# Output projection in another pass order, decode attention per key/value pair, and a wider warm-up, in one hybrid trunk layer

## The chip, the cores and the metric

The kernel runs on one core of a Trainium2 chip. TensorE multiplies (its weights are loaded by a queue of its own, PEld), VectorE (DVE), ScalarE (ACT) and GpSimd (POOL) do the elementwise work, and DMA queues, most of them issued from SyncE (SP), bring weights from HBM. The metric is the device time of one execution in microseconds; the median of three runs before the change is 2037.36 us (2037.23 to 2038.41).

## The reference

One layer for 256 prompt tokens and 8 sample tokens (one each of 8 sequences), 264 columns together:

```python
x = x + 0.5 * swiglu(rmsnorm(x, n1), f1g, f1u, f1d)          # FFN1, d_ff 5504
proj = rmsnorm(x, nm) @ w_in                                  # 2048 -> q, k, v and RWKV columns
o_att, k_buf, v_buf = attend(q, k, v, sinks)                  # 16 query heads, 4 kv heads of 64
o_rwkv, shift, S = rwkv_time_mix(proj[..., ATT_COLS:], shift0, wkv0, ...)   # 16 heads of 64
x = x + concatenate([o_att, o_rwkv]) @ w_out
x = x + 0.5 * swiglu(rmsnorm(x, n2), f2g, f2u, f2d)          # FFN2
y = rmsnorm(x, final_norm)
```

For the prompt, `attend` is sliding-window attention (window 128) with a relative bias per head and a sink per head:

```python
s = einsum('...qhgd,...khd->...hgqk', q, k) * 64**-0.5 + bias
m = maximum(max(s), sink);  p = exp(s - m)
o = einsum('...hgqk,...khd->...qhgd', p / (sum(p) + exp(sink - m)), v)
```

For the sample tokens the same formula runs against a cache of 128 keys and values per sequence, with the token's own key and value appended as column 129 (`swa_decode`). `rwkv_time_mix` is a recurrence with a 64x64 state per head, a group norm per head and a gate.

## The kernel before

Activations lie transposed: a tile is 128 features by 264 tokens. The model width has 16 tiles (`KD`), the FFN 43, the input projection 38. Each large product ("GEMM") is done in two-part fp32: `chunk` (L116-125) loads 256 KB of weights by SP, ACT casts them to `hi` (L123), DVE subtracts to `lo`; then three matmuls of 128x264 per 128x128 weight block go into an accumulator `acc` (three PSUM buffers, `NACC`). The raw weights have a ring of six, `hi` and `lo` rings of four. All other matmuls write to "m" banks (five, `mp()`).

The program is written as generator tasks: `spawn` makes one, `tick` (called by `gemm` between weight blocks) steps the open tasks, `drain(list)` steps until the tasks of the list are done. A scheduler then orders each engine's instructions; each engine runs its own order from first to last, and so do the DMA queues. What is queued behind a waiting instruction waits too.

The mixing stage runs in the order of `SEQ`: four batches of RWKV heads ("b", two pairs of heads each), keys and values ("kv"), then eight query tiles q0 to q7. The work that runs beside the input projection and after it:

- `chain`, one per batch: a triangular solve in 32 steps (DVE on X and Xt), a round trip of Xt through DRAM (`sb`, then `TT`), small matmuls (names TN, zs, W, BT, gm, uv, N, S), and at the end `gnorm`, a group norm with a Sqrt on ACT and two reciprocals on DVE. Batch b gives the mixed tiles 2b and 2b+1.
- `attend(t, q)` (L712-753), one per query tile t: for each of two heads, matmuls of scores, a custom DVE step that adds the bias and takes the maximum (L730), `softmax` (L701-710: exponentials on ACT, the sum and the division on DVE), then three transposes (L739-741), and the product with the values. Tile t gives mixed tile 8+t; p = t // 4 is the key/value pair.
- `dec_attend(att)` (L755-819), one task for all sample tokens, spawned after q7: scores with cached keys as weights and padded queries of 8 columns as moving data, the softmax of 129 columns, values likewise; at the end it waits for all eight attention tasks and copies its columns into the mixed tiles 8 to 15 by POOL (L818).

The output projection (L867-881) goes over the 16 mixed tiles in passes, given by the table `PASS` (L40): tiles 0-3, then 4-7, then 8-15. Before each pass `drain(need(ks))` completes what its tiles depend on; `split` casts the tiles to `hi` and subtracts `lo` (L857-861); for each of 16 output blocks one accumulator then takes 3 matmuls for every tile of the pass, and DVE adds it to the residual `xr`. The last pass hands its sums to FFN2. `need` (L863) counts any tile above 7 as needing all attention tasks and the decode.

At the very start TensorE runs 14 fp32 matmuls of 128x128 on a tile of ones (`NWARM`), which need only a memset.

Of the kernel before, what the change touches and what calls it, by code (L numbers as in the profile page):

```python
# [7 lines left out]
F32 = mybir.dt.float32  # L8
# [22 lines left out]
NWARM = 14  # L31
# [8 lines left out]
PASS = [[0,1,2,3],[4,5,6,7],[8,9,10,11,12,13,14,15]]  # L40
# [3 lines left out]
NVEC = 155  # L44
# [3 lines left out]
def body(tc, I, O):  # L48
# [24 lines left out]
    def mm(out, lhsT, rhs, start=True, stop=True, **k):  # L73
        TE.matmul(out, lhsT, rhs, start=start, stop=stop, **k)  # L74
# [20 lines left out]
    with ExitStack() as ctx:  # L95
# [17 lines left out]
        def mp():  # L113
            return pp.tile([P, 512], F32, tag="m", bufs=NM, name=uid("m"))
# [37 lines left out]

        warm = mp()
        for _ in range(NWARM):
            mm(warm[:, :P], ones, ones)
# [176 lines left out]
        def mixing_body(mx, n2, n3, XD):  # L332
            def fix(shape, name):
                return mx.tile(list(shape), F32, name=name)
# [23 lines left out]
            qd = fix((P, 2, NB, 4), "qd")  # L358
# [353 lines left out]
            def attend(t, q):  # L712
                p = t // 4
                G.tensor_copy(qd[:, p, :, t % 4], q[:, NP:T])
# [40 lines left out]
            def dec_attend(att):  # L755
                yield
                qb = tmp((P, 2, NB, 2, 4))
                G.memset(qb, 0.0)
                for h in range(2):
                    r = HALF[h]  # L760
                    G.tensor_copy(qb[r, :, :, h, :], qd[r])
                yield
                sps = mp()
                sv = sps[:, :P].rearrange("p (h x) -> p h x", h=2)
                for p in range(2):
                    for b in range(0, NB, 2):
                        kc = load(I["kc"][p, b // 2], (P, 2, P))
                        for j in range(2):
                            c0 = p * 32 + (b + j) * 4
                            mm(sv[:, :, c0:c0 + 4], kc[:, j, :], qb[:, p, b + j])  # L770
                st = tmp((P, P))
                A.copy(st, sps[:, :P])
                pr = tmp((P, 2, NB, 4))
                for p in range(2):
                    tt(G, pr[:, p], qd[:, p], bc(kT[p][:, NP:T].unsqueeze(2), (P, NB, 4)), ALU.mult)
                yield
                s2 = mp()
                TE.transpose(s2[:, 0:P], st, ident)
                for h in range(2):
                    r = HALF[h]  # L780
                    mm(s2[r, P:P + 1], pr[r], ones[r, 0:1])
                bd = load(I["bd"], (P, 129))
                s = tmp((P, 129))
                mxv = ring((P, 2), "mxv", 6)
                V.tensor_tensor_reduce(out=s, in0=s2[:, 0:129], in1=bd, op0=ALU.add, op1=ALU.max, scale=1.0,
                                       scalar=vc(VSD), accum_out=mxv[:, 0:1])
                softmax([s], mxv, vc(VSD), 1)
                dg = tmp((P, P))
                ts(V, dg, ident, s[:, P:P + 1], ALU.mult)
                yield  # L790
                tp = mp()
                TE.transpose(tp[:, 0:P], s[:, 0:P], ident)
                pt = tmp((P, P))
                A.copy(pt, tp[:, 0:P])
                pn = mp()
                for h in range(2):
                    r = HALF[h]
                    mm(pn[r, 0:64], ones[:, 0:64], dg[:, r])
                od = tmp((P, 2, NB, 4))
                for p in range(2):  # L800
                    tt(V, od[:, p], pn[:, p * 32:p * 32 + 32].rearrange("p (b i) -> p b i", i=4),
                       bc(vT[p][:, NP:T].unsqueeze(2), (P, NB, 4)), ALU.mult)
                yield
                op = mp()
                ov, pv = (x[:, :P].rearrange("p (h x) -> p h x", h=2) for x in (op, pt))
                for b in range(NB):
                    vcache = load(I["cv"][b], (P, 256))
                    for p in range(2):
                        c0 = p * 32 + b * 4
                        mm(ov[:, :, c0:c0 + 4], vcache[:, p * P:(p + 1) * P], pv[:, :, c0:c0 + 4])  # L810
                of = od.rearrange("p a b i -> p (a b i)")
                for h in range(2):
                    r = HALF[h]
                    tt(V, of[r], ov[r, h, :], of[r], ALU.add)
                while any(g in tasks for g in att):
                    yield
                for t in range(8):
                    G.tensor_copy(mixed[8 + t][:, NP:T], od[:, t // 4, :, t % 4])  # L818
# [5 lines left out]
            bat, att, bts = [], [], []  # L824
            for kind, i in SEQ:
# [10 lines left out]
                elif kind == "kv":  # L836
                    w, p = i // 2, i % 2
                    ps = win(LKV + i)
                    x = slot()
                    (kT, vT)[w][p] = x  # L840
                    with tc.high_priority():
                        tt(V, x, ps[:, :T], rs, ALU.mult)
                    spawn(kvtask(w, p, x))
                else:
                    ps = win(LKV + 4 + i)
                    q = slot(tag="o")
                    with tc.high_priority():
                        stt(q, ps[:, :T], 0.125, rs, ALU.mult, ALU.mult)
                    att.append(spawn(attend(i, q)))
                    if len(att) == 8:  # L850
                        att.append(spawn(dec_attend(list(att))))
# [11 lines left out]
            def need(ks):  # L863
                return [g for i, g in enumerate(bat) if any(k // 2 == i for k in ks)] + (att if max(ks) > 7 else [])
# [93 lines left out]
def layout(i):  # L958
# [3 lines left out]
    for n in (1, 2):  # L962
# [9 lines left out]
    heads = np.array([(2 * p + h) * 4 + j for h in range(2) for p in range(2) for b in range(NB) for j in range(4)])  # L972
# [4 lines left out]
        np.broadcast_to(i["attn_sinks"][0], (P, 16)), i["attn_sinks"][0][heads][:, None]], 1))  # L977
# [20 lines left out]
    a["kc"] = c(ck.reshape(4, 2, P, 2, P).transpose(3, 0, 4, 1, 2))  # L998
# [30 lines left out]
```

## Time and profile before

| | |
|---|---|
| median of 3 runs | 2037.36 us |
| profiled execution, span | 2034.2 us |
| DVE, ACT, POOL busy | 1324.9, 1035.9, 241.2 us |
| HBM read, written | 347.25 MB, 10.21 MB |
| first projection matmul | 1099.96 us |
| first FFN2 matmul into an "m" bank | 1268.07 us |

The profile is one execution. Its span is the device work of that execution and is 3.2 us shorter than the median, which is taken around the whole launch. The views used are the page (busy time by engine, the chain of waits that ended last), the timeline of an engine (start, duration, engine, line, operation, out<-in, form, count), and busy times by stage. In a stage's row stand the stretch, its length, the busy time and count of each engine, the clock that TensorE was granted (1.00 is full), the busy share of the DMA engines and GB/s.

### The profile page before, as it was taken

The page shows a single profiled execution, that of the slowest core. Times are in us where ns is not written, and L with a number is a line of the kernel's source. Part 1 is how long each engine was busy: PE and PEld are TensorE (multiplying, and loading weights), DVE is VectorE, ACT ScalarE, POOL GpSimd, SP SyncE. Part 2 cuts the span into 40 slices and gives each one's busy share as a digit, 9 for nine tenths or more (in the row PEclk, how much of TensorE's full clock was granted, in tenths as well). Part 3 has the DMA queues.
Part 4 walks back from the last instruction along what each step waited for, and adds up shares of the span by engine and source line. Part 5 has one row for each costly group of instructions (what it writes and reads, how often), then busy time and mean ns, then how long its engine had stood idle before and what let it go on. Part 6 is the DMA issues. An engine that isn't in the chain of part 4 may idle for free.

```text
span 2034.2 us, 45416 instructions
## 1 busy us (share of the span) xinstructions
PE 2000.0 (98%) x17096; PEld 1963.2 (97%) x17096; DVE 1324.9 (65%) x2647; ACT 1035.9 (51%) x2027; POOL 241.2 (12%) x337
## 2 busy tenths in 40 slices
PE   9999999999999999999999999999999999999998
PEld 9999999999999999999898789999999999999998
DVE  5865555655555577678778756775666666666665
ACT  5644444444444466665555534554444444444445
POOL 0301001020110122120100000120101101010012
PEclk9999999999999999999999979999999999999999
DMA  6566565655556576554455335465565565656654
GB/s 228 177 187 197 180 195 186 187 184 176 186 171 191 181 208 204 153 153 125 138 146 165 101 108 180 172 183 177 191 182 193 182 189 187 189 191 180 194 182 145
DMA packets 227421, 358.39 MB, mean 176 GB/s; under 512 B 42352, under 2 KB 80768, under 8 KB 227200
## 3 DMA queue, kind: packets, MB, share of 16 engines
q1 hardware_dynamic: 220752, 346.95, 54.7%
q10 hardware_dynamic: 6448, 8.53, 1.3%
q8 instruction: 134, 2.20, 0.4%
q14 instruction: 87, 0.71, 0.1%
HBM read 347.25 MB, written 10.21 MB: 176 GB/s over the span
## 4 chain that ended last, share of the span: by engine, by line
PE 93%; DVE 3%; DMA 1%; ACT 1%; issue 1%; SPq 1%; ACTq 0%; DVEq 0%
PE acc L74 84%; PE m L74 8%; DVE lo L58 1%; DMA raw<-in_win 1%; ACT t L68 0%; DVE y L58 0%; ACT L68 0%; DVE st L58 0%; DVE Xt L58 0%; DVE t L678 0%; DMA ld<-in_sT 0%; ACT hi L123 0%; DMA raw<-in_gu 0%; SPq L544 0%; PE m L496 0%
## 5 line engine op out<-in xcount | busy, mean ns | idle before, releaser
L58 DVE TENSOR_TENSOR lo<-raw,hi 128x512 fp32r<-128x512 f32 (+1 forms) x1288 | 869.8, 679 | 549.0 <-ACT hi L123 522.3
L123 ACT CAST hi<-raw 128x512 fp32r<-128x512 f32 (+1 forms) x1288 | 776.4, 607 | 865.1 <-PE acc L74 777.2
L74 PE MATMUL acc<-s,hi 128*128 128x264 f32 x5940 | 1109.8, 286 | 3.9 <-ACT hi L123 2.1
L74 PEld LDWEIGHTS acc<-s,hi 128*128 128x128 f32 x5940 | 923.7, 189 | 11.3 <-ACT hi L123 2.5
L74 PE MATMUL acc<-s,lo 128*128 128x264 f32 x2970 | 847.9, 286 | 4.4 <-DVE lo L58 4.4
L74 PEld LDWEIGHTS acc<-s,lo 128*128 128x128 f32 x2970 | 559.8, 189 | 7.7 <-DVE lo L58 5.2
L74 PE MATMUL acc<-t,hi 128*128 128x264 f32 x2752 | 503.0, 284 | 0.0
L74 PEld LDWEIGHTS acc<-t,hi 128*128 128x128 f32 x2752 | 426.3, 188 | 0.0
L74 PE MATMUL acc<-t,lo 128*128 128x264 f32 x1376 | 388.9, 285 | 0.0
L58 POOL TENSOR_TENSOR t<-t,t 128x264 f32<-128x264 f32 (+1 forms) x148 | 150.8, 1019 | 1151.4 <-ACT hi L123 791.1
L74 PEld LDWEIGHTS acc<-t,lo 128*128 128x128 f32 x1376 | 258.4, 188 | 0.1
L74 PE MATMUL acc<-y,hi 128*128 128x264 f32 x648 | 124.5, 285 | 0.0
L74 PEld LDWEIGHTS acc<-y,hi 128*128 128x128 f32 x648 | 101.7, 188 | 0.2
L74 PE MATMUL acc<-y,lo 128*128 128x264 f32 x324 | 92.4, 285 | 0.0
L58 DVE TENSOR_TENSOR t<-acc,t 128x264 f32<-128x264 f32 x156 | 67.4, 432 | 37.0 <-PE acc L74 36.8
L58 POOL TENSOR_TENSOR o<-o,o 128x264 f32<-128x264 f32 x43 | 36.1, 840 | 231.6 <-ACT o L68 227.6
L74 PE MATMUL acc<-o,hi 128*128 128x264 f32 x324 | 63.0, 284 | 0.0
L74 PEld LDWEIGHTS acc<-y,lo 128*128 128x128 f32 x324 | 60.8, 188 | 0.0
L61 DVE SCALAR_TENSOR_TENSOR s<-acc,s 128x264 f32<-128x264 f32 x96 | 40.6, 427 | 15.9 <-PE acc L74 15.5
L74 PEld LDWEIGHTS acc<-o,hi 128*128 128x128 f32 x324 | 50.3, 188 | 0.0
L74 PE MATMUL m<-s,hi 128*128 128x264 f32 x260 | 48.6, 285 | 0.0
L61 DVE SCALAR_TENSOR_TENSOR x<-acc,x 128x264 f32<-128x264 f32 x96 | 40.5, 427 | 10.0 <-PE acc L74 9.6
(236 smaller groups left out, 1301.1 us busy)
## 6 DMA issues: line engine op xcount, KB each, us to landing
raw<-in_gu SPq DMA_DIRECT2D x688, 256.0 KB, 3.3
raw<-in_dn SPq DMA_DIRECT2D x224, 256.0 KB, 2.8
raw<-in_win SPq DMA_DIRECT2D x152, 256.0 KB, 3.4
raw<-in_dn SPq DMA_DIRECT2D x160, 192.0 KB, 2.7
raw<-in_wout SPq DMA_DIRECT2D x64, 256.0 KB, 3.3
xsp<-x ACTq DMA_DIRECT2D x16, 132.0 KB, 3.3
s<-xsp SPq DMA_DIRECT2D x16, 132.0 KB, 4.0
ld<-in_sT SPq DMA_DIRECT2D x16, 128.0 KB, 3.3
```

Source lines behind the costliest of these rows:

```text
L58: return e.tensor_tensor(out=out, in0=a, in1=b, op=op)
L61: return V.scalar_tensor_tensor(out=out, in0=a, scalar=s, in1=b, op0=op0, op1=op1)
L74: TE.matmul(out, lhsT, rhs, start=start, stop=stop, **k)
L123: A.copy(hi[:, :w], raw[:, :w])
```

## The change

Three things are changed.

1. The warm-up: a memset of 640 columns of ones, a DVE copy of 512 of them into a tile of the `hi` ring, and 44 matmuls with 512 to 128 columns each (f32r), instead of 14 fp32 matmuls of 128x128.
2. The pass order: `PASS` is now tiles 0-3 with 8-11, then 4-7, then 12-15, and `need` lists what each tile needs by itself. The first pass needs batches 0 and 1, attention tiles 0-3 and the decode of pair 0; each of its output blocks takes 24 matmuls; the last pass takes 12.
3. The decode attention runs once per key/value pair, as two tasks, with the queries padded to 32 columns as the weights and the cache (128 columns) as the moving data. Cache tiles of a whole pair (512 KB each) are loaded ahead into another ring, for pair 0 after batch 2 and for pair 1 after decode 0 and batch 3. The new value's share is added from a DRAM copy of the new values (`vnd`).

```diff
-NWARM = 14
+WARM = (512,) * 6 + (384,) * 6 + (264,) * 8 + (256,) * 8 + (192,) * 8 + (128,) * 8
-PASS = [[0,1,2,3],[4,5,6,7],[8,9,10,11,12,13,14,15]]
+PASS = [[0,1,2,3,8,9,10,11],[4,5,6,7],[12,13,14,15]]
+        G.memset(C, 1.0)
+        wr = wp.tile([P, CH * P], F32R, tag="hi", bufs=NHL, name=uid("hi"))
+        V.tensor_copy(wr, C[:, :CH * P])
         warm = mp()
-        for _ in range(NWARM):
-            mm(warm[:, :P], ones, ones)
+        for n in WARM:
+            mm(warm[:, :n], wr[:, :P], wr[:, :n])
+                    if w:
+                        A.dma_start(vnd, kvn[w])
+                        while bat[-2] in tasks:
+                            yield
+                        dec_load(0)
...
+            def dec_load(p):
+                dk[p], dv[p] = ring((P, NB, P), "uv", NUV), ring((P, NB, P), "uv", NUV)
...
+                SP.dma_start(dk[p], I["kc"][p])
+                SP.dma_start(dv[p], I["cw"][p])
+                SP.dma_start(db[p], I["bd"][p])
...
+            def dec_attend(p, qs):
+                for i, q in enumerate(qs):
+                    for h in range(2):
+                        G.tensor_copy(qb[p][HALF[h], :, h * 4 + i], q[HALF[h], NP:T])
...
+                for b in range(NB):
+                    g, x = b % 4 * 32, b // 4 * 129
+                    mm(sps[g:g + 32, x:x + P], qb[p][:, b], dk[p][:, b])
+                for b in range(NB):
+                    g, x = b % 4 * 32, b // 4 * 129 + P
+                    mm(sps[g:g + 32, x:x + 1], qb[p][:, b], kT[p][:, NP + b:NP + b + 1])
...
+                softmax([s[:, 0], s[:, 1]], mxv, vc(VSD + p), 2)
...
+                for j in range(2):
+                    TE.transpose(tp[:, j * P:(j + 1) * P], s[:, j, 0:P], ident)
...
+                for b in range(NB):
+                    g, j = b % 4 * 32, b // 4
+                    mm(op[g:g + 32, j * P:(j + 1) * P], pt[:, j, g:g + 32], dv[p][:, b])
+                for j in range(2):
+                    stt(oa[:, j], vr[p][:, j], s[:, j, P:P + 1], op[:, j * P:(j + 1) * P], ALU.mult, ALU.add)
...
+                for i, q in enumerate(qs):
+                    G.tensor_copy(q[:, NP:T], od[:, i])
+                if p == 0:
+                    while bat[-1] in tasks:
+                        yield
+                    dec_load(1)
...
+                    att.append([spawn(attend(i, q))])
+                    if i % 4 == 3:
+                        p = i // 4
+                        d = spawn(dec_attend(p, qs[4 * p:]))
+                        for a in att[4 * p:]:
+                            a.append(d)
             def need(ks):
-                return [g for i, g in enumerate(bat) if any(k // 2 == i for k in ks)] + (att if max(ks) > 7 else [])
+                return [bat[k // 2] for k in ks if k < 8] + [g for k in ks if k > 7 for g in att[k - 8]]
```

How it moves the instructions, at three places. First ACT, around the start of the projection; the casts of L859 (L873 in the changed kernel) make the projection's inputs from the mixed tiles `y`, and the activations with `sta` and `stc` are the exponentials of attention tile 0. Before:

```order
L68 ACTIVATE t_15109<-m_15184,eps 128x264
L123 CAST hi_16571<-raw_16570 128x512
L859 CAST s_16392<-y_12692 128x264
L859 CAST s_16396<-y_12693 128x264
L859 CAST s_16400<-y_13753 128x264
L859 CAST s_16404<-y_13754 128x264
L68 ACT_TABLE_LOAD
L68 ACTIVATE t_15207,stb_15213<-t_15207,sta_15212 128x256
```

and of the change:

```order
L123 CAST hi_16694<-raw_16693 128x512
L68 ACT_TABLE_LOAD
L68 ACTIVATE t_15240,stb_15246<-t_15240,sta_15245 128x256
L68 ACTIVATE t_15241,stb_15246<-t_15241,sta_15245 128x128
L68 ACTIVATE stc_15247<-sta_15245,vec 128x2
L68 ACTIVATE t_15292,stb_15298<-t_15292,sta_15297 128x256
L68 ACTIVATE t_15293,stb_15298<-t_15293,sta_15297 128x128
L68 ACTIVATE stc_15299<-sta_15297,vec 128x2
L873 CAST s_16506<-y_12725 128x264
```

The four casts now stand behind the exponentials of both heads. Second, DVE at the same place: `sta` is the negated maximum that these exponentials take as their bias, and TT is what batch 3's solve brings back from DRAM. Before:

```order
L730 ISA mxv_15261 128x1
L58 TENSOR_TENSOR y_14805<-m_15107,t_15109 128x264
L65 TENSOR_SCALAR sta_15212<-mxv_15209 128x2
L61 SCALAR_TENSOR_TENSOR y_14804<-y_14804,vec,t_12817 128x264
L58 TENSOR_TENSOR Xt_14687<-Xt_14687,st_15249 128x8x2
```

and of the change:

```order
L58 TENSOR_TENSOR y_14838<-m_15141,t_15143 128x264
L58 TENSOR_TENSOR TT_14729<-TT_14729,C 32x8x32
L65 TENSOR_SCALAR sta_15245<-mxv_15242 128x2
L58 TENSOR_TENSOR TT_14729<-TT_14729,C 32x8x32
L61 SCALAR_TENSOR_TENSOR y_14837<-y_14837,vec,t_12850 128x264
L58 TENSOR_TENSOR TT_14729<-TT_14729,C 32x8x32 x2
L65 TENSOR_SCALAR sta_15297<-mxv_15294 128x2
```

The last steps of the solve (Xt) now stand ahead, and the additions on TT have come between the maximum and its negation. Third, TensorE where the first pass goes on after attention tile 3 (rows 8616 on of 15618). Between the first halves of three accumulators and this place stands no GEMM matmul from row 8530 on:

```order
L74 MATMUL m_16118<-sgl,ld_15983 128x264
L74 MATMUL m_16122<-sgl,ld_15985 128x264
L745 MATMUL m_16126<-C,t_15912 128x128
L746 MATMUL m_16126<-C,t_15911 128x128
L747 MATMUL m_16126<-C,t_15911 128x128
L819 MATMUL m_16134<-C,t_16075 128x128 x2
L74 MATMUL m_16177<-t_16062,s_14815 64x256
L74 MATMUL m_16177<-t_16130,s_14815 64x256
L74 MATMUL acc_16538<-s_16522,hi_16570 128x264
L74 MATMUL acc_16618<-s_16522,hi_16694 128x264
L74 MATMUL acc_16718<-s_16522,hi_16742 128x264
```

The rows with `sgl` are the gate of batch 3 behind its group norm, L819 the last transposes of the first decode task; the accumulators' second halves (mixed tiles 8 to 11) follow them. From there to the first FFN2 matmul into an "m" bank stand 768 GEMM matmuls, 348 of them up to the end of the first pass, with attention tiles 4-7 and the second decode task (32 score and value matmuls, transposes) among the 348.

More of the change, by code (lines that the diff above doesn't have):

```diff
@@ L771, in dec_attend @@
[L771 to L775, printed above, removed]
-                yield
[L777 to L782, printed above, removed]
@@ new lines, in dec_attend @@
+                for b in range(NB):
+                    g, x = b % 4 * 32, b // 4 * 129 + P
+                    mm(sps[g:g + 32, x:x + 1], qb[p][:, b], kT[p][:, NP + b:NP + b + 1])
+                dm = ring((P, 768), "bk", 2)
+                s = dm[:, 0:258].rearrange("p (s x) -> p s x", s=2)
+                pt = dm[:, 258:514].rearrange("p (s x) -> p s x", s=2)
+                od = dm[:, 514:546].rearrange("p (i b) -> p i b", i=4)
+                mxv = ring((P, 2), "mxv", 6)
+                for j in range(2):
+                    V.tensor_tensor_reduce(out=s[:, j], in0=sps[:, j * 129:j * 129 + 129], in1=db[p], op0=ALU.add,
+                                           op1=ALU.max, scale=1.0, scalar=vc(VSD + p), accum_out=mxv[:, j:j + 1])
@@ L803, in dec_attend @@
+                A.copy(pt, tp[:, 0:2 * P].rearrange("p (s x) -> p s x", s=2))
                 yield
                 op = mp()
-                ov, pv = (x[:, :P].rearrange("p (h x) -> p h x", h=2) for x in (op, pt))
                 for b in range(NB):
[L807 to L811, printed above, removed]
@@ L812, in dec_attend @@
-                for h in range(2):
[L813 to L818, printed above, removed]
+                    g, j = b % 4 * 32, b // 4
+                    mm(op[g:g + 32, j * P:(j + 1) * P], pt[:, j, g:g + 32], dv[p][:, b])
+                oa = tmp((P, 2, P))
@@ L971, in layout @@
     sc = cols[:NSH * P] - 1536
-    heads = np.array([(2 * p + h) * 4 + j for h in range(2) for p in range(2) for b in range(NB) for j in range(4)])
+    heads = np.array([[(2 * p + min(x // 4, 1)) * 4 + x % 4 for g in range(4) for x in range(32)] for p in range(2)])
     a["vec"] = c(np.concatenate([
```

65 lines of the change are left out of this document (25 added, 40 removed).

## Prediction

> **What bounds the kernel now.** I read the shares by engine first, then the chain of waits, then the busy times by stage. The page's first and fourth parts:
>
> ```profile
> PE 2000.0 (98%) x17096; PEld 1963.2 (97%) x17096; DVE 1324.9 (65%) x2647; ACT 1035.9 (51%) x2027; POOL 241.2 (12%) x337
> PE 93%; DVE 3%; DMA 1%; ACT 1%; issue 1%; SPq 1%; ACTq 0%; DVEq 0%
> ```
>
> TensorE sets the time, and 98% busy leaves 34 us. But a busy TensorE is not one at full rate, so the stages matter. Two rows of the chain give the price of one GEMM matmul (128x264), the second where FFN2 takes over:
>
> ```profile
> 69.33 700.36 PE acc L74 x5760
> 1268.07 7.30 PE m L74 x60
> ```
>
> 700.36/5760 = 0.1216 us. The stretch that the change rearranges runs from the first projection matmul to FFN2's first one at 1268.07. The first is the first row here (timeline); the others are busy times by stage (PE, weight loads, DVE, ACT, POOL, then the granted clock, DMA share and GB/s):
>
> ```profile
> 1099.96 0.93 PE L74 MATMUL acc<-s,hi 128*128 128x264 f32 x4
> ...
> 1099.96:1146.41 46.45, 45.41 (x530) 40.13 (x529) 39.44 (x139) 24.66 (x74) 2.15 (x3) 1.00 0.50 145
> 1146.41:1157.45 11.04, 7.44 (x33) 4.60 (x32) 8.48 (x24) 7.60 (x21) 0.65 (x1) 0.73 0.15 45
> 1157.45:1188.27 30.82, 30.82 (x224) 26.48 (x224) 24.45 (x89) 17.45 (x52) 1.52 (x6) 0.99 0.43 132
> 1188.27:1214.56 26.29, 22.97 (x116) 18.77 (x114) 8.06 (x31) 6.57 (x22) 1.91 (x10) 0.58 0.35 99
> 1214.56:1268.07 53.51, 53.51 (x420) 53.51 (x421) 35.49 (x60) 25.23 (x46) 2.65 (x3) 0.95 0.47 161
> ```
>
> These are 168.1 us for 768 projection matmuls and 36 of the last input projections, 804 in all: 97.8 us at 0.1216. Some 70 us go to attention, batch 3 and decode. Two holes stand out: 11.0 us in which batch 3 reaches its group norm, and 26.3 us in which TensorE is "busy" with the decode's thin matmuls and the last attention tiles at a clock of 0.58. The last row is 420 matmuls in 53.51 us, 0.127 each, because it begins at half clock. The change attacks both holes, and pays for it at the start.
>
> **The warm-up.** Before, TensorE opens with 28 passes of the 14 square matmuls, and DVE is idle until 7.68. Real work is dense from 15.9:
>
> ```profile
> 0.73 0.20 POOL L147 MEMSET ones<- 128x128 f32 x1 [0.29 <-POOLq L1021]
> 0.99 5.12 PE L74 MATMUL m<-ones 128*128 128x128 f32 x28 [0.99 <-POOL eps L150]
> 8.21 1.03 PE L74 MATMUL acc<-s,hi 128*128 128x264 f32 x4 [2.10 <-ACT hi L123]
> ...
> 11.25:15.90 4.65, 4.43 (x35) 1.00 0.97 358
> 15.90:26.10 10.20, 10.20 (x84) 1.00 0.72 214
> ...
> 1106.23 0.11 PE m L740
> 1156.05 0.21 PE m L740
> ```
>
> Up to 15.9, 56 GEMM matmuls are done (4 of them slower), so at the dense pitch of 10.20/84 = 0.1214 the head equals dense work from about 15.9 - 52 x 0.1214 = 9.6. The new warm-up needs a memset of 640 columns (the 128-column one takes 0.20 with its fixed part; about 0.6 by size), then a DVE copy (about 0.5, as a 128x264 step takes 0.4 to 0.5), so it starts near 2.15 rather than 0.99. Its 44 matmuls stream 6x512 + 6x384 + 8x(264+256+192+128) = 12,096 columns; at 264 per 0.12 us that is 5.5 us, 6.1 with a fixed part each, 11.5 if all ran at half clock. The last two rows are one pass of 128 columns at full and at half clock: 0.11 and 0.21; 28 passes in 5.12 us are then about 20 at half clock, 4 us. With 4 us at half rate the new one ends near 10.15: 0.5 us after the equivalent 9.6. Bounds: 8.25 (nothing lost) to 13.65, when a backlog of ready chunks limits the loss to 1.8. I take **+0.5** (0 to +1.8). The ring tile it borrows is one of four; chunks wait for inputs until 8.2 anyway.
>
> **The new order: stretch A, up to the second half of the first pass.** The order of TensorE shows it: three accumulators take their first halves (36 matmuls, rwkv tiles 0-3) as before, then all four attention tiles 0-3, batch 3 and decode 0 must come before the next one. Until then TensorE has no GEMM to fill with. So A is a path over DVE and ACT, and I walked it from rows of before.
>
> (a) Its start. ACT's order now has the exponentials of tile 0 ahead of the four casts that feed the projection, and DVE's has the first softmax steps behind the batch's TT additions, which wait for a DRAM round trip:
>
> ```profile
> 1097.72 1.34 ACT L859 CAST s<-y 128x264 fp32r<-128x264 f32 x4
> 1099.08 1.28 ACT L68 ACT_TABLE_LOAD   x1
> 1104.25 0.28 ACT L68 ACTIVATE stc<-sta,vec 128x2 f32<-128x2 f32 x1
> ...
> 1104.72 2.56 SPq L544 DMA_DIRECT2D sb<-Xt  x4
> 1110.51 0.41 DVE L58 TENSOR_TENSOR TT<-TT,C 32x256 f32<-32x256 f32 x1
> ```
>
> The round trip takes 5.8 us (1104.72 to 1110.51). In the new order the solve Xt ends ahead of both reciprocals of batch 2, near 1097.5 by my estimate (its last steps stood around 1096 to 1104 among them), so TT is there near 1103.3. Two heads of exponentials (2.2 us on ACT) bring 1106, the casts 1.34: the first projection matmul moves from 1099.96 to about **1107.5**. A loss of 7.5 us at the front, which has only 36 matmuls to place, so it is not on the path: DVE is.
>
> (b) The heads. Tile 1 begins near 1110. One head on DVE, and the next one's beginning:
>
> ```profile
> 1142.07 0.48 DVE L730 CUSTOM_DVE_ANT_0 t<-m,ld,vec 128x256 f32<-128x256 f32 x1
> 1142.86 0.17 DVE L65 TENSOR_SCALAR sta<-mxv 128x2 f32<-128x2 f32 x1
> 1144.70 0.15 DVE L58 TENSOR_TENSOR stb<-stb,stc 128x2 f32<-128x2 f32 x1
> ...
> 1145.76 0.47 DVE L730 CUSTOM_DVE_ANT_0 t<-m,ld,vec 128x256 f32<-128x256 f32 x1
> ```
>
> 3.69 us, of which 1.7 (1143.03 to 1144.70) are the round over ACT; batch 3's steps fill that gap. Six heads (tiles 1-3): 22.1 us, to 1132.3. Steps of batch 3 too long for the gaps add about 3: decode 0's softmax begins near 1135.4.
>
> (c) Decode 0's softmax is that of one head with two halves of 129 columns and two exponentials; its one-column predecessor took 1199.16 to 1201.15, two halves with the queue behind batch 3 about 5.4:
>
> ```profile
> 1199.16 0.35 DVE L785 CUSTOM_DVE_ANT_0 t<-m,ld,vec 128x129 f32<-128x129 f32 x1 [2.61 <-PE m L74]
> 1200.86 0.29 DVE L65 TENSOR_SCALAR t<-t,stb 128x129 f32<-128x129 f32 x1
> 1148.23 1.28 ACT L68 ACT_TABLE_LOAD   x1
> 1149.53 0.85 ACT L68 ACTIVATE t<-m,eps 128x264 f32<-128x264 f32 x2
> 1150.04 3.46 DVE L678 RECIPROCAL t<-t 128x264 f32<-128x264 f32 x2 [1.10 <-ACT t L68]
> ```
>
> To 1140.8. Then batch 3's group norm, 1148.23 to 1153.50 = 5.3 us: 1146. Behind it decode 0 still has the additions of the new V (two of about 0.3), two transposes, two copies, four POOL copies of 0.14 and the casts of the mixed tiles:
>
> ```profile
> 1211.53 0.46 DVE L58 TENSOR_TENSOR t<-m,t 64x64 f32<-64x64 f32 x2 [2.16 <-PE m L74]
> 1212.05 1.10 POOL L818 COPY o<-t 128x8 f32<-128x8 f32 x8 [33.73 <-DVE t L58]
> 1213.27 2.60 ACT L859 CAST s<-o 128x264 fp32r<-128x264 f32 x8
> ```
>
> Before, that same tail took 1211.53 to the first GEMM matmul near 1213.7; with the transposes and four casts about 6.5: A ends near **1152.5** at full clock.
>
> (d) The clock. Two-us windows of before:
>
> ```profile
> 1152.00:1154.00 2.00, 0.29 (x1) 0.29 (x2) 2.00 (x5) 0.00 (x0) 0.00 (x0) 0.50 0.00 0
> 1194.00:1196.00 2.00, 2.00 (x12) 2.00 (x11) 1.07 (x3) 0.62 (x1) 0.00 (x0) 0.50 0.49 166
> ...
> 1188.60 2.30 PE L74 MATMUL m<-t,ld 128*128 128x8 f32 x20
> 1202.78 5.13 PE L74 MATMUL m<-t,ld 128*128 128x8 f32 x24
> ```
>
> It falls to 0.50 after a few idle us, and also with TensorE fully busy on thin work: 0.21 a matmul in place of 0.115. Batch 3's chain has some 250 small matmuls in A (4.2 us for 120 at full clock); if half of them, the transposes and the decode's 32 are at half clock, A grows by 2 to 4 us. I take 2: **1154.5**. Bounds: 1150 (DVE's own work in A, 41 us from 1107.5, with few gaps) and 1163 (every step at half clock, and softmax 0 queued behind batch 3).
>
> The Trainium skill (TensorE: Matmul & The Clock Gate, Part 1: The HAM clock gate) states that an idle window of about 3.4 us halves the clock, and as long a busy one restores it. The idle row at 1152 agrees with it; the row at 1194 shows half clock with TensorE counted busy, so here the trace goes beyond the page. By the page alone A, never wholly idle that long until late, would keep full clock and the sum would be 2 us lower; by the row at 1194 it would not.
>
> **Stretch B: to the end of the first pass.** 348 GEMM matmuls, tiles 4-7, decode 1, without a hole. The nearest row is the GEMM with attention beside it:
>
> ```profile
> 1164.00:1188.00 24.00, 24.00 (x183) 21.14 (x184) 19.95 (x68) 14.49 (x44) 1.43 (x5) 1.00 0.52 156
> 1164.00:1188.00 24.00, 19.17 (x142) 17.72 (x143) 5.12 (x12) 0.00 (x0) 1.00 0.52 156
> ```
>
> The second row is the accumulators alone: 142 matmuls, 17.3 us at 0.1216, so 6.7 us are the other 41, some 1.86 tiles: 3.6 us a tile. B: 348 x 0.1214 = 42.2; the rest of tile 4, 2.6; tiles 5-7, 10.8; decode 1 about 4 (8 score and 8 value matmuls of 128 columns, two passes of 0.11 each, 3.5, and 4 transposes; up to 6 if the 8 of one column cost two passes of 0.115 each, down to 2.3 if their 32-column weights go partly side by side, which no row shows); 1 for stalls and half clock at its start. Together **60.6** (57 to 64).
>
> **Then dense.** 420 matmuls to FFN2's: 420 x 0.1216 = **51.1** instead of 53.51, as they now follow a busy TensorE.
>
> The removed parts cost nothing more: 16 cache loads of 128 KB are replaced by 4 of 512 KB, DMA at half share throughout; the order of FFN1 and of nearly all of the input projection is the same, so nothing there moves.
>
> **The sum.** 1154.5 + 60.6 + 51.1 = 1266.2 against 1268.07: -1.9; +0.5 at the head: -1.4. The profiled span is 2034.2, 3.2 below the median 2037.36, which is timed around it; the same is taken after: span 2032.8, time **2036.0**.
>
> **Rivals.** *The first pass starves (slower).* The first pass now waits for the last batch and decode 0, and nothing fills TensorE meanwhile. For: A's rows are a path over DVE, ACT and DRAM without spare work, a walk leaves waits out rather than in, and half clock was seen with thin work. Against: batch 3 was the bound of a hole before, too. If A ends at 1162 or later, decode 1 costs 6, and B starts cold: 1162 + 62 + 51.1 = 1275.1, +7.0, head +0.5 or +1: about 2045. It decides from A's end above 1160 with B at 60.6 (1160 + 60.6 + 51.1 = 1271.7, +3.6, head +0.5 = +4.1): then the whole is measurably slower than before.
>
> *The walls fall (faster).* A at 1150, near DVE's busy sum, decode 1 hidden at 2.3: 1150 + 58 + 51 = 1259, -9.1, head +0.5: 2028.8. For: hole two, 26.3 us, holds only 12 GEMM matmuls, and the decode that made it now runs behind 348. Against: 41 of 46 us of DVE in A without queueing.
>
> *The edit moves the wait only (same).* Waiting goes from before the last pass to before the first and the sums agree to a microsecond or two; time 2037. Only the warm-up would then tell.
>
> **How the numbers follow.** What a measurement can tell from no change is about 0.2%, 4.1 us. My forecast (a gain of 1.4, its own range 2031 to 2041) has 0.40: same 0.26, faster 0.09, slower 0.05. Starving 0.30: slower 0.27, same 0.03. Walls 0.24: faster 0.24. Moved only 0.06: same 0.05, faster 0.01. So faster 0.34, same 0.34, slower 0.32. The range of 8 in 10 takes in the walls and the starving case: 2027 to 2046.
>
> **What would show it.** A right: one hole of TensorE between the 36 first-half matmuls and the next accumulators, ending at 1152 to 1157, with DVE above 80% busy in it; B 60 us with no hole, decode 1 in it; the last 420 at 0.1216 and clock 1.00. The head: warm-up ending near 10, then the first chunks with no wait. Wrong: a second hole in B, A ended by a DMA (sb, TT, the broadcast of new V), or FFN1 and the input projection shifted.

## The result, and the profile after

The changed kernel takes 2028.85 us (median of 5 runs, 2028.04 to 2030.71) against 2037.36: a ratio of 0.9963, with a 95% interval of 0.995 to 0.9975. That is 7.5 us less, between 5.1 and 10.2 (the medians alone lie 8.5 apart). It is faster by more than the 0.2% that can be told from no change. The time is inside the range of the prediction, but the forecast was 2036.0, a gain of 1.4. Run again later (e11), the ratio was 0.9962 (0.9948 to 0.9975). The profiled execution has a span of 2027.1 us, 7.1 less than before. It is 1.75 us shorter than its own time around the launch, and in all other runs of this case that difference is 1.7 to 1.9 (in e3's up to 2.15). So the 3.2 us between span and median before are not the launch alone: the profiled execution of the kernel before was itself some 1.4 us shorter than the median.

Busy time by engine and the shares of the chain, from the page of the changed kernel:

```profile
PE 1990.2 (98%) x17142; PEld 1954.5 (96%) x17142; DVE 1329.2 (66%) x2659; ACT 1039.3 (51%) x2038; POOL 243.0 (12%) x343
PE 90%; DVE 4%; DMA 3%; SPq 1%; issue 1%; ACT 1%; POOL 0%; DVEq 0%; ACTq 0%; POOLq 0%
```

TensorE is as busy as before, 10 us less in total. The chain now has DMA at 3%: around the start of the projection it runs through a round trip that TensorE waits for. Where the projection begins, on TensorE's timeline, and then the busy times by stage (PE, weight loads, DVE, ACT, POOL, clock, DMA share, GB/s):

```profile
1099.47 0.71 PE L74 MATMUL m<-sgl,ld 128*128 128x264 f32 x2 [0.75 <-DVE mxv L736]
1107.59 0.81 PE L74 MATMUL acc<-s,hi 128*128 128x264 f32 x2 [7.41 <-ACT s L873]
...
1099.57:1107.59 8.02, 0.61 (x2) 0.19 (x2) 6.11 (x20) 2.69 (x12) 0.00 (x0) 0.60 0.79 213
1107.59:1140.45 32.86, 28.59 (x394) 23.03 (x395) 23.02 (x102) 18.20 (x64) 1.45 (x2) 0.89 0.34 105
1140.45:1151.60 11.15, 9.53 (x50) 6.62 (x50) 9.19 (x27) 6.19 (x16) 3.02 (x14) 0.73 0.19 54
1151.60:1211.70 60.10, 60.10 (x482) 53.09 (x482) 41.40 (x126) 33.30 (x93) 4.39 (x10) 0.99 0.40 121
1211.70:1262.85 51.15, 51.15 (x423) 51.15 (x423) 40.85 (x76) 24.94 (x43) 0.95 (x1) 1.00 0.53 181
```

The reader is to see three things. TensorE idles 7.4 us at the beginning, for the casts. The second halves of the first accumulators begin at 1151.60, after a stretch in which the clock is down twice. Then 111 us run without a hole to FFN2's first matmul, at 1262.85 instead of 1268.07. The 26.3 us at clock 0.58 before the last pass are gone.

So 5.2 us of the 7.1 are won between the projection and FFN2. FFN1 begins within 0.1 us of where it did. Another 1.65 us appear in FFN2, whose instructions were not changed; the two chains, before and after:

```profile
1406.63 615.17 PE acc L74 x5040
```

```profile
1400.99 613.52 PE acc L74 x5040
```

The same 5040 matmuls take 615.17 and 613.52 us. That is a pitch of 0.1221 against 0.1217, at a granted clock of 1.00 in both.

### The profile page after: what moved, and what is told of

The parts are those of the page before. It is cut to its first block, busy times and chain, and to the rows that moved or that the text cites. A ratio compares the mean times of both kernels' runs of the same rounds, so it can differ in the third digit from the quotient of the medians.

```text
span 2027.1 us, 45546 instructions
## 1 busy us (share of the span) xinstructions
PE 1990.2 (98%) x17142; PEld 1954.5 (96%) x17142; DVE 1329.2 (66%) x2659; ACT 1039.3 (51%) x2038; POOL 243.0 (12%) x343
## 4 chain that ended last, share of the span: by engine, by line
PE 90%; DVE 4%; DMA 3%; SPq 1%; issue 1%; ACT 1%; POOL 0%; DVEq 0%; ACTq 0%; POOLq 0%
PE acc L74 82%; PE m L74 7%; DVE lo L58 1%; DMA raw<-in_win 1%; DMA TT<-sb 1%; DMA sb<-Xt 0%; DVE t L680 0%; DVE st L58 0%; SPq L530 0%; DVE Xt L58 0%; DVE y L58 0%; ACT L68 0%; DMA Xt<-sa 0%; DMA raw<-in_wout 0%; ACT t L68 0%
```

## The experiments

Two questions were open: which of the three parts makes the gain, and what bounds the stretch before 1151.6. My theory: the decode's new form, with its tasks behind other work, and dense matmuls afterwards make the gain; the warm-up does nothing. The rivals: the pass order makes it, or the warm-up, or the half clock holds the rest. All ratios are to the kernel before, run beside each kernel on the same chip. The last column is from the one profiled execution of each kernel. Executions of one kernel lie up to 8 us apart (e11: 2027.09 to 2035.07), so a difference of a few us in that column is no result by itself; e9's is its longest execution, the kernel before's a short one.

| run | what it is | ratio, 95% interval | FFN1's start to FFN2's start, us |
|---|---|---|---|
| (before) | | | 1198.7 |
| (changed) | | 0.9963 (0.9950-0.9975) | 1193.6 |
| e1 | warm-up alone | 0.9999 (0.9990-1.0007) | 1202.4 |
| e2 | decode and warm-up, old passes | 0.9938 (0.9923-0.9952) | 1187.7 |
| e3 | passes alone | 1.0109 (1.0090-1.0128) | 1222.4 |
| e4 | changed, other passes | 0.9935 (0.9921-0.9950) | 1190.9 |
| e5 | changed, 64 filler matmuls | 0.9969 (0.9957-0.9980) | 1197.4 |
| e6 | changed, batch 3's norm late | 0.9965 (0.9953-0.9978) | 1193.3 |
| e7 | before, no decode | 0.9920 (0.9905-0.9935) | 1186.2 |
| e8 | changed, no decode | 0.9929 (0.9915-0.9942) | 1186.2 |
| e9 | e2, casts early | 0.9936 (0.9924-0.9949) | 1190.4 |
| e10 | changed, 30 filler matmuls | 0.9969 (0.9958-0.9981) | 1196.3 |
| e11 | changed, again | 0.9962 (0.9948-0.9975) | 1194.0 |
| e12 | decode alone | 0.9950 (0.9935-0.9964) | 1190.0 |

**e1, the warm-up alone.** The kernel before with

```diff
-NWARM = 14
+WARM = (512,) * 6 + (384,) * 6 + (264,) * 8 + (256,) * 8 + (192,) * 8 + (128,) * 8
```

and the memset, copy and loop that go with it.

> The kernel before with the new warm-up alone. If the gain sits in the projection (as the traces say: FFN2 begins 5.2 us earlier, FFN1 begins within 0.1 us), the time stays at 2037 within 1 us, and the chain of waits again has FFN1's 5760 matmuls from 69.3. If the wider warm-up is worth what lies outside the projection, it comes out about 2 us lower, 2035. The trace also decides on FFN2's pitch: before, 5040 matmuls of it took 615.17 us, in the changed kernel 613.52. If that difference belongs to one execution or one program's layout, it will differ here too; if it belongs to the change of the mixing stage, 615.2 comes back.

Measured: no change. FFN2's 5040 matmuls took 613.50 us, so the shorter time appears without the change of the mixing stage. But the trace shows an effect that I had not counted: a hole of 7.2 us in front of the first projection matmul, which the kernel before does not have.

```profile
1112.29 1.42 PE L74 MATMUL acc<-s,hi 128*128 128x264 f32 x4 [7.22 <-ACT s L862]
```

In this kernel, too, ACT's order has the four casts behind the exponentials of attention tile 0. The warm-up is at the other end of the program, and the only edit; the scheduler came to another order a thousand microseconds later. Batch 3's solve stands earlier in it: the additions on TT begin at 1108.2, and at 1110.5 in the kernel before.

**e2, the old pass order.** The changed kernel with

```diff
-PASS = [[0,1,2,3,8,9,10,11],[4,5,6,7],[12,13,14,15]]
+PASS = [[0,1,2,3],[4,5,6,7],[8,9,10,11,12,13,14,15]]
```

> The changed kernel with the pass order of before (tiles 0-3, then 4-7, then 8-15), so the decode per pair and the warm-up alone. If the pass order makes the gain, the first hole (11.0 us, batch 3 before the second pass) comes back and the time is near the kernel before, 2034 to 2037. If it is the decode's new form that matters (no thin matmuls at half clock before the last pass: 26.3 us with 12 GEMM matmuls in it before), the second hole shrinks below 10 us, FFN2 begins 10 us or more before 1268 and the time is 2022 to 2028, better than the changed kernel, whose first stretch to 1151.7 has only 36 GEMM matmuls.

Measured: 0.9938, as the theory expected, and lower than the changed kernel's 0.9963; the two intervals overlap by 0.0002 only. The first place below is the start, the second where the hole of 11.0 us was before, the third the neighbourhood of the last pass (busy times by stage):

```profile
1101.30:1108.98 7.68, 0.60 (x2) 0.19 (x2) 6.10 (x20) 2.69 (x12) 0.00 (x0) 0.78 0.77 215
1164.00:1168.00 4.00, 2.33 (x16) 1.54 (x15) 3.41 (x15) 3.96 (x12) 1.67 (x7) 1.00 0.74 201
1204.00:1213.00 9.00, 7.40 (x63) 5.50 (x63) 4.01 (x8) 3.56 (x11) 2.22 (x6) 1.00 0.33 104
```

Besides the 7 us at the start, 1.7 and 1.6 us of idle TensorE are left, at full clock. The second hole closed without the new pass order, and the first one nearly so.

**e3, the pass order alone.** The opposite edit of `PASS` in the kernel before.

> The kernel before with the new pass order alone; its one decode task then must be done, with all eight attention tiles, before the first pass. By my theory the order gains only because the decode of pair 0 can be had by itself: here every wait stands before the first GEMM, DVE's some 110 us of attention, batch 3 and decode cannot lie under TensorE, and 768 matmuls (93 us) follow without cover: FFN2 begins at 1285 to 1305, time 2055 to 2075. If the order of the passes were good in itself, it would be below 2037.

Measured: 22 us slower, in the lower half of what I expected. The first row is the stretch up to the first pass, the second the rest:

```profile
1104.00:1197.51 93.51, 69.89 (x547) 52.72 (x545) 49.82 (x215) 36.75 (x132) 3.60 (x15) 0.74 0.24 67
1197.51:1292.70 95.19, 95.19 (x770) 95.08 (x771) 69.37 (x123) 45.31 (x81) 5.46 (x6) 0.98 0.57 172
```

The projection's 768 matmuls all lie in the second; attention, batch 3 and the decode lie in the first without them. The order pays only with a decode that can be had by halves.

**e4, three other passes.** The changed kernel with

```diff
+PASS = [[0,1,2,3],[4,5,8,9,10,11],[6,7,12,13,14,15]]
```

> The changed kernel with passes 0-3, then 4, 5 and 8-11, then 6, 7 and 12-15: the first pass is short again and needs no attention, while no pass but the last needs batch 3 and decode 1. If the stretch to 1151.7 is costly because TensorE has nothing to do there (36 matmuls in 52.7 us), 192 of the 768 now lie in it and FFN2 begins 8 to 12 us earlier: 2017 to 2022. If DVE is the bound there (its busy time was 138 of the 164 us from 1099 to 1263), the chunks that are added to that stretch push attention and decode back, and the gain is 0 to 4 us: 2025 to 2029.

Measured: 0.9935, 13 us less than the kernel before, some 6 less than the changed one. That is between the two expectations. (DVE's busy time in the changed kernel from 1099 to 1263 was 121 of 164 us, not the 138 of the expectation.) It has idle time from 1103 to 1114 and from 1166 to 1174.

**e5 and e10, a filler for the clock.** In the changed kernel, for pair 0 only:

```diff
                 if p == 0:
+                    fm = mp()
+                    for _ in range(40):
+                        mm(fm[:, :P], fl, fl)
...
                 if p == 0:
+                    for _ in range(24):
+                        mm(op[:, 2 * P:3 * P], fl, fl)
```

`fl` is a constant tile of 128x128; nobody reads the results. The counts are those of e5; e10 has 20 and 10.

> The changed kernel with 64 matmuls of 128x128 on a constant tile, whose results nobody reads, put on TensorE where it waits in the first decode: 40 ahead of the transposes of its softmax (TensorE idle for 3.0 us there), 24 behind its value matmuls (idle 1.45 us). The granted clock fell to 0.50 from 1145 to 1152.5, and TensorE's chain of 6.2 us from 1145.44 to 1151.6 ran at it. If the clock is what holds up the end of that stretch, it ends 2.5 to 3.5 us earlier and the time falls as much, to 2025 to 2026.5 beside 2028.9 of the changed kernel. If DVE holds it (79 to 83% busy there), nothing changes within 1 us.

> e5 again with fewer matmuls: 20 and 10 instead of 40 and 24, since one took 0.117 us and 64 of them were in the way. 2.3 and 1.2 us now fit into the idle time. If the half clock from 1145 to 1152.5 costs the changed kernel time, 2 to 3 us go, to a ratio of 0.995 to the kernel before. If what the stretch gains is given back after it, as in e6, the ratio stays at 0.9955 to 0.997.

Measured: both 0.9969, no gain. The clock did what it was to do. TensorE's row from 1140 to 1152, of the changed kernel, then of e10, and e10's timeline:

```profile
1140.00:1152.00 12.00, 9.93 (x52) 7.02 (x53) 10.00 (x29) 6.93 (x18) 3.42 (x14) 0.73 0.18 51
```

```profile
1140.00:1152.00 12.00, 9.96 (x77) 7.66 (x76) 9.71 (x29) 6.74 (x19) 2.20 (x9) 1.00 0.13 40
...
1139.43 2.45 PE L74 MATMUL m<-fl 128*128 128x128 f32 x20
1142.59 0.30 PE L812 MATMUL m<-C,bk 128*128 128x128 f32 x1 [0.71 <-DVE bk L65]
1149.78 0.38 PE L828 MATMUL m<-C,t 128*128 128x128 f32 x2
1153.91 1.41 PE L74 MATMUL acc<-s,hi 128*128 128x264 f32 x4 [2.29 <-ACT s L882]
```

From the first transpose to the decode's last ones (1142.59 to 1149.78) it takes 7.2 us, where the changed kernel took 9.0 (1140.45 to 1149.46): full clock is worth 1.8 us there. But behind them the first GEMM matmul waits for ACT's casts, 4.1 us after the last transposes instead of 2.1. A table load and tile 4's exponentials, which the changed kernel has done by 1148.95, come in e10's order behind a copy that waits for TensorE, and end at 1152.84. And the fall of the clock is not gone, it comes later, onto the projection's own matmuls:

```profile
1153.36:1160.18 6.82, 6.27 (x27) 5.43 (x28) 3.74 (x14) 3.77 (x13) 2.82 (x7) 0.50 0.21 68
```

What the clock gave, ACT's order and the later half clock took. In e5, too, it is at 0.50 for 3.4 us behind the filler (from 1155.8), and the filler was too long: 40 matmuls took 4.68 us and ended after DVE was ready.

**e6, batch 3's group norm later.**

```diff
+                if bt.i == 3:
+                    yield from pause(6)
                 gps = []
```

> The changed kernel with the group norm of batch 3 put off by six task steps, so that its two reciprocals (3.46 us on DVE from 1141.78) come behind the first decode's additions of the new V (1145.64), which stood queued behind them with their value matmuls done at 1143.2. Batch 3 is not needed before the second pass. If this queueing is a part of the 52.7 us that I priced at 5.3 us, the first pass goes on 3 to 5 us earlier and the time falls by as much, to 2024 to 2026, since DVE is busy 41 of 60 us afterwards. If DVE's sum of work is the bound in both stretches, it comes out within 1 us of 2028.9.

Measured: 0.9965, no change. The second halves begin at 1150.39 instead of 1151.60, and the stretch behind is 60.97 us instead of 60.10:

```profile
1098.00:1150.39 52.39, 38.88 (x456) 29.04 (x456) 37.54 (x147) 25.68 (x90) 4.95 (x17) 0.84 0.42 124
1150.39:1211.36 60.97, 60.94 (x490) 54.23 (x490) 44.95 (x132) 36.04 (x98) 3.58 (x9) 1.00 0.43 122
```

The two reciprocals went out of the decode's way (its additions moved from 1145.64 to 1143.88), and of those 1.8 us 1.2 arrived; 0.9 were given back.

**e7 and e8, no decode.** The tasks of the decode and their loads are left out of the kernel before and of the changed one; the attention of the sample tokens is not computed.

> The kernel before without its decode task: the attention of the sample tokens is left out. If the second hole (26.3 us, 12 GEMM matmuls in it) is the decode's price, 20 to 24 us go and the time is 2014 to 2018. If attention tiles 4 to 7 would make most of that hole anyway, 8 to 12 go: 2026 to 2030.

> The changed kernel without its two decode tasks and their loads, so again without the attention of the sample tokens. The first pass then waits for attention tiles 0-3 alone, while batch 3 is free to come later. By my sum decode 0 has 5.4 us of softmax and 6.5 us of tail in the first stretch, the second decode 4 us: 10 to 16 us go, to 2013 to 2019. If the new decode is nearly free where it stands, the time is 2024 to 2028. The difference of the two kernels without decode tells what the pass order is worth by itself: by my sum the new order is 0 to 5 us slower.

Measured: 0.9920 and 0.9929. Both lie between their two expectations: with 2037.36 for the kernel before they are 2021.1 and 2022.9 us. Without a decode the two kernels are alike within their intervals, and alike from FFN1's start to FFN2's, 1186.2 us both. So the decode cost the kernel before 0.8%, 16 us, and the changed kernel 0.34 points, 7 us. This difference of 9 us, from different sets of runs and with intervals of some 3 us on each ratio, is the whole gain, as far as these runs can tell. What was left of the second hole in e7:

```profile
1172.00:1256.72 84.72, 84.69 (x664) 78.73 (x663) 61.23 (x157) 46.15 (x106) 2.79 (x3) 1.00 0.52 152
```

Nothing: 84.7 us at full clock without idle time. So the decode made that hole. Its 26.3 us are not its price, though: attention tiles and 12 projection matmuls lay in them too, and only 12.5 us (by the trace) to 16 (by the ratio) went with it.

**e9, the casts early.** In the kernel of e2, the splits of the first pass's tiles are put ahead of the loads of the residual:

```diff
+            drain(need(PASS[0]))
+            with tc.high_priority():
+                for k in PASS[0]:
+                    split(k)
             xr = [slot() for _ in range(KD)]
```

> The kernel of e2 (new decode, old pass order), in which the casts of the first pass's four tiles no longer stand behind the residual's loads for their buffers and behind the first exponentials: they are made during the input projection. In e2 TensorE idled from 1102 to 1110 for them. If that hole is on the path, FFN2 begins 5 to 8 us earlier than in e2 and the time is 2019 to 2022. If DVE's work is the bound of the whole region, the time is that of e2, 2025 to 2028.

Measured: 0.9936, as e2. The hole at the start is gone (first row); in its place come 3 us of idle time and a clock of 0.68 where batch 3 ends (second):

```profile
1100.00:1108.00 8.00, 8.00 (x55) 7.30 (x55) 7.15 (x17) 3.48 (x6) 0.00 (x0) 1.00 0.72 194
1152.00:1168.00 16.00, 13.00 (x64) 8.98 (x63) 12.27 (x44) 9.85 (x29) 2.99 (x11) 0.68 0.28 83
```

**e11, the changed kernel again.**

> The changed kernel again beside the two others. The ratio to the kernel before should be 0.995 to 0.9975 again. Its trace shows how much one kernel's stretches differ between executions: FFN2's 5040 matmuls took 613.5 us, and 615.2 in the kernel before; the first stretch's end stood at 1151.7. If these repeat within 1 us they belong to the program; if FFN2 comes to 614 or more, or the stretch ends 2 us elsewhere, single traces cannot carry differences of 2 us.

Measured: 0.9962. FFN2's 5040 matmuls took 613.52 us again; FFN1 began 1.2 us later (70.48), and from there to FFN2 it took 1194.0 us instead of 1193.6. Between the two they differ by more: counted from FFN1's start, the first transpose of the decode comes 1.0 us later, and the half clock behind it lasts 3.4 us instead of 6.8. So these two traces agree within 1 us, and FFN2's time repeats; but the five runs of this kernel lie 8 us apart, and no trace shows the longer ones.

**e12, the decode alone.** The changed kernel with the old warm-up and the old passes.

> The kernel before with the decode per pair alone: old warm-up, old pass order. In e2 (the same with the new warm-up) the casts that begin the projection stand behind the exponentials of tile 0 and TensorE idles from 1102 to 1110; with the old warm-up the casts stand ahead of them, as in the kernel before. If that hole is paid in time, this is 3 to 7 us faster than e2, 2020 to 2024, a ratio of 0.990 to 0.992. If what is won there is lost at a later wait, as e6, e9 and e10 showed for other holes, the ratio is that of e2, 0.992 to 0.995; then the decode's new form is the whole gain, and the new pass order gives part of it back. FFN2's 5040 matmuls will take 613.5 us if their pitch goes with the old warm-up's absence, and 615.2 if with its presence.

Measured: 0.9950, 10 us less than before, and no faster than e2; the expected 3 to 7 us did not come. As in e9 the start is filled but for 1.9 us of idle time, and where batch 3 ends 4 us are idle at a clock of 0.74:

```profile
1100.00:1108.00 8.00, 6.12 (x39) 5.08 (x38) 8.00 (x28) 5.33 (x17) 1.44 (x2) 1.00 0.95 302
1154.00:1172.00 18.00, 14.05 (x73) 10.16 (x73) 12.88 (x36) 9.30 (x27) 5.25 (x16) 0.74 0.14 41
```

FFN2 took 614.98 us in it. Over the thirteen programs it was between 613.50 and 615.73, with the new warm-up (613.50 in e1, 614.11 in e4, 615.73 in e2) as without (613.78 in e7, 614.15 in e3, 615.17 before). Which side of the decode's new form pays (the swapped roles of weights and moving data, the two tasks or the loads ahead) was not separated.

## Why the prediction held, and where it was off

The range of 2027 to 2046 held the time. The likeliest case, a gain of 1.4 us that cannot be told from nothing, did not come: the measured gain is 7.5, and the chance that I gave to a measurable one was 0.34. The sum missed 2028.85 by 7.1 us, and the misses all point one way: 2.9 us at the end of stretch A, 0.6 at the head, 0.5 in stretch B, 1.65 in FFN2, and 1.45 in the 3.2 us that it adds to the span, which measured 1.75.

*The head.* The warm-up was to end near 10.15 and ended at 10.00; its memset and copy took 0.63 and 0.43 against 0.6 and 0.5. The cost of +0.5 was not there: FFN1 began at 69.25, and at 69.33 before. Over all traces it began at 69.19 to 70.48 with the new warm-up and at 69.33 to 70.53 with the old, so nothing of it shows. What I missed is the warm-up's other effect, on the order at 1100 (e1).

*Stretch A, (a) to (d).* I put its end at 1154.5; it stood at 1151.60. Its steps, in turn: the first projection matmul at 1107.5, measured 1107.59; the end of decode 0's softmax 1140.8, measured 1140.6; the end of batch 3's reciprocals 1146, measured 1145.24:

```profile
1140.11 0.48 DVE L65 TENSOR_SCALAR bk<-bk,stb 128x129 f32<-128x129 f32 x2
1141.78 3.46 DVE L680 RECIPROCAL t<-t 128x264 f32<-128x264 f32 x2 [1.19 <-ACT t L68]
1145.64 0.59 DVE L61 SCALAR_TENSOR_TENSOR t<-bk,bk,m 128x128 f32<-128x128 f32 x2
```

These hits are in part luck. ACT was done with the exponentials near 1107.2 instead of 1106, but the first matmul began 0.4 us later, behind one cast, and not behind all four (1.34). Tile 1's first head began on DVE at 1112.04 and not near 1110, and the last head was done at 1139.70 instead of 1135.4. Decode 0's softmax, which I put behind the heads with 5.4 us, ran beside the last one from 1136.81 on, and so made this good:

```profile
1112.04 0.48 DVE L736 CUSTOM_DVE_ANT_0 t<-m,ld,vec 128x256 f32<-128x256 f32 x1 [0.83 <-PE m L74]
1136.81 0.35 DVE L799 CUSTOM_DVE_ANT_0 bk<-m,bk,vec 128x129 f32<-128x129 f32 x1
1139.15 0.55 DVE L65 TENSOR_SCALAR t<-t,stb 128x256 f32<-128x256 f32 x2
```

e8 shows that (c) had the path wrong there. Without any decode, batch 3's reciprocals end at 1146.41, no earlier than with it:

```profile
1142.94 3.47 DVE L680 RECIPROCAL t<-t 128x264 f32<-128x264 f32 x2 [1.10 <-ACT t L68]
```

So decode 0's softmax does not push the group norm. What the two kernels have in common, the heads of attention and batch 3's chain, sets it.

The term that was mis-sized is (c)'s tail. I gave it 6.5 us at full clock and (d) 2 more for the half clock; both together it took 6.4, from 1145.24 to 1151.60. The half clock, from 1145.6 to 1152.4 (it was there from 1101.2 to 1114.9, too), costs 1.8 us by e10, near the 2 of (d); but the decode's value matmuls and first transposes, to which (d) gave it, ran at 1.00. So the tail is worth some 4.6 us at full clock by this estimate, not 6.5. In e8 the same place, at full clock and without a decode, takes 4.9 (1146.41 to 1151.26): the decode's own steps add little to it. The 7 us that it cost lie mostly behind, where e8 needs 53.3 us to the end of the first pass and the changed kernel 60.1; 27 more of the first pass's matmuls are already done in e8 by then.

*Stretch B*: 60.6 forecast, 60.1 measured, without a hole. *Dense*: 51.1 forecast, 51.15 measured. FFN2 begins 5.2 us earlier where I had 1.4; that is A's end, the head and stretch B (rounded).

*Decode 1.* I priced its score and value matmuls at two passes of 0.11 each, and held open 2.3 us in all, if their 32-column weights go side by side. The low price is the right one: decode 0's eight value matmuls, 16 passes, took 0.65 us, 0.08 a matmul and not 0.22. That they go side by side is not shown; the 16 weight loads of 32 columns also took only 0.38 us, where e5's 40 loads of 128 columns took 4.54. So B's total was hit with a term some 2 us too large in it, and what took its place was not followed up. The row from the changed kernel:

```profile
1142.51 0.65 PE L74 MATMUL m<-uv,bk 128*32 128x128 f32 x16 [0.16 <-ACT bk L807]
```

*"Nothing moves in FFN1 and FFN2."* FFN1's chain is 700.36 us in both kernels. FFN2's became 1.65 us shorter; that step failed, as the sum had no term for it. It is a property of the program and not of the execution: e11 repeats it to 0.01 us, and e5, e6, e8 and e10, which keep the three parts, have 613.52 too. No single part decides it, as e1 has 613.50 and e2, with the same warm-up, 615.73. Its cause stays open; where the buffers of FFN2 come to lie was not tried.

*The rivals.* "The walls fall" gave 2028.8 and named hole two as the reason, which e7 and e8 bear out; its numbers for A (1150) and B (58) were lower than what came. That its time meets the measured one is luck: it has FFN2 begin 3.4 us too early, and FFN2's 1.65 and the 1.45 at the launch make up for most of it. "The first pass starves" has its mechanism shown by e3, where it costs 22 us, but not in this kernel. The new pass order is no source of the gain: without a decode it changes nothing that can be told (0.9920 and 0.9929), with the new decode the old order is as good or better (0.9938 against 0.9963). That it costs 5 us is likely, not settled. I had looked for the gain in the order of passes, and it lay in the decode.

*The clock.* The Trainium skill (TensorE: Matmul & The Clock Gate, Part 1: The HAM clock gate) states that the clock goes to half after at least one idle window of about 3.4 us. The traces go beyond it. The first two rows are the 3.4 us ahead of the two falls in the changed kernel, the others those ahead of the two in the kernel before:

```profile
1097.81:1101.22 3.41, 1.62 (x7) 0.67 (x5) 3.41 (x11) 1.25 (x1) 0.00 (x0) 1.00 0.61 144
1142.18:1145.59 3.41, 1.80 (x23) 1.20 (x22) 3.41 (x4) 1.86 (x4) 0.00 (x0) 1.00 0.01 2
1148.10:1151.52 3.42, 2.00 (x13) 1.35 (x11) 2.25 (x5) 3.37 (x6) 0.00 (x0) 1.00 0.01 3
1189.06:1192.48 3.42, 3.42 (x26) 2.55 (x25) 2.28 (x9) 1.29 (x6) 0.00 (x0) 1.00 0.65 156
```

In the first three TensorE was idle for about half of the time, in pieces of at most 1.5 us. So the idle row at 1152, which the prediction took as agreement with the Trainium skill, does not show it: the clock was at 0.50 from 1151.52, when TensorE had been idle for 0.2 us. In the fourth TensorE is counted as busy throughout, with the decode's 20 matmuls of eight columns among the work (2.30 us); the same 20 matmuls precede a fall in e1, and in e7, without the thin matmuls, the last 84.7 us stayed at 1.00. That a half idle stretch or thin work is enough fits these traces; neither was tried by itself. The prediction also called A "never wholly idle that long until late", beside its own loss of 7.5 us at the front. TensorE was idle there for 7.4 us.

## What to carry to other kernels

A wait that goes from one place often comes back at another: e6, e9, e10 and e12 each shortened or closed a wait of 2 to 7 us and gained nothing that can be told. That fits a bound behind it in the chain of batch 3 and attention, which e8 leaves where it was; shortening that chain itself was not tried. Taking work out of that region (the decode's 16 us become 7) is what paid. The price of a part is read best by leaving it out of both kernels, before its stages are summed up; and where a scheduler orders the program, an edit at one end can reorder the other, so the order is to be compared over the whole program.

The best version here is the new decode with other passes: e2, e4 and e9 are at 0.9935 to 0.9938, 13 us below the kernel before.

## What was not expected of the hardware

The same 5040 matmuls at the same granted clock took 613.5 to 615.7 us in different programs, and 613.52 twice in one program. Matmuls of 128x128 in this number format, back to back, took 0.117 us each (4.68 us for 40, e5) at full clock, hardly less than the 0.1216 of those with 264 columns; their weight loads alone took 4.54 us. The half clock lasted 13.65 and 6.82 us in the changed kernel's stretch A, 13.65 and 3.41 in its second trace, and 6.82 and 27.30 in the kernel before: multiples of 3.41.
